# Matmuls of different parts of the TensorE array issued as neighbours in the mixers of a hybrid layer

## The chip, the core and the metric

The kernel runs as one program on one core of a Trainium2 chip. The metric is the device time of one execution in microseconds; less is better. A core has TensorE (matrix products, with an array of 128 rows by 128 columns), VectorE, ScalarE, GpSimd, SyncE (which issues most DMAs) and 16 DMA engines. In the views TensorE's products are PE, its weight loads PEld, VectorE is DVE, ScalarE is ACT, GpSimd is POOL, SyncE is SP. Each engine runs its own instructions in the order in which they were issued to it.

## What is computed

One layer of a diffusion backbone, all in f32: 512 latent tokens and 256 context tokens of width 1024.

```
mod      = silu(c) @ w_mod + b_mod                 # 6 x 1024: shifts, scales, gates
h        = rmsnorm(x) * (1 + sc1) + sh1            # latent and context
cols     = h @ w_in                                # 4480 columns
y_rw     = RWKV-7, 8 heads of 64, both directions  # s = s*w + (s a) b + v k ; y = s r
y_hg     = HGRN2, 8 heads of 64, both directions   # gated linear attention in blocks of 32
x        = x + g1 * (concat(y_rw, y_hg) @ w_out)
h2       = rmsnorm(x) * (1 + sc2) + sh2
x        = x + g2 * (shared SwiGLU(h2) + sum of 8 of 64 routed SwiGLU experts(h2))
out      = rmsnorm(x)
```

Each latent scan begins with the final state of the context scan of its direction.

## The kernel before, in words

Two parts follow one another. The *mixers* take x to `x1` (projection, RWKV-7, HGRN2, output product). The *experts* then route the tokens and stream 64 experts' weights through on-chip buffers.

**The mixers** are generator functions ("streams") that issue instructions step by step; a `yield` ends a step. A planner (`run`) walks over the streams and gives every step a priority worked out from the table `PLAN`: for each stream some due times and, as last number, how many steps it has. A stream's steps are spread evenly over its due times; instructions then stand on each engine in the order of their priorities. The streams are W and P (weight split, projection), E (conv and evacuation), O (RWKV operands), S (RWKV scores, `rw_scores`), I (inverse of small triangles), A, B and C (chains, `rw_chain`), H and K (HGRN2 pairs, `hgrn_pair`), M (rest of the modulation, `s_mod`), N and U (RWKV output, output product).

Heads go in pairs: a tile's 128 partitions hold head 0 of the pair in rows 0 to 63 and head 1 in rows 64 to 127. j counts the four pairs, d the two directions, n the twelve 64-token chunks (4 of context, 8 latent).

- `rw_scores` (L687 matmul, L689 mask and copy on VectorE): for each (j, d) and two chunks, one head after the other: two matmuls of 64 rows, a step; the mask multiply, a step; then the other head; then the DMAs. The two heads use two PSUM banks in turn.
- `rw_chain`: per chunk n, the first product into pR (L888: 64x64 matmuls of W and the scores, two heads; L891: full-height product with the state S, for n > 0), once for each direction; the copy Rs; the U product (L902, direction outside, head inside); the copy W; the state product (L910) and its update; in the latent chunks the output product pY (L926 with S, L928 with W), again once for each direction.
- `hgrn_pair`: for each direction, two groups of 256 tokens and two heads, one step with six matmuls into one bank: p0 (L1115) and p1 (L1116) of 64 rows by 128 columns, p2 (L1118) of 64 by 64, in turn for i = 0 and 1; a step with a predicated copy (L1122); a step with three copies on ScalarE (L1127, L1129). The next head takes the other bank.
- `s_mod`: w_mod's columns 2048 to 6143 in eight blocks m of 512; four loads of 512 KB each (256 rows by 512 columns), and for each load two matmuls of 128 rows by 32 columns on strip g of the array's columns, 512 columns wide.

An f32 matmul stands in the trace as two weight loads and two products; "pieces" are those products.

Of the kernel before, what the change touches and what calls it, by code (L numbers as in the profile page):

```python
# [46 lines left out]
def hybrid_layer(ctx, tc, x, c, xctx, c_ctx, w_mod, b_mod, norm1_g, norm2_g, w_in, rw_conv, rw_w0, rw_w2,  # L47
# [3 lines left out]
    nc = tc.nc  # L51
# [620 lines left out]
    def rw_scores(j, d):  # L672
# [4 lines left out]
        for n in range(0, NCH, 2):  # L677
            lat = n >= NCC
            m = n - NCC if lat else n
            w = WCT[lat]  # L680
            na = w // 64
            st = xq.tile([128, 2, 2, 2, 64], F32, name="SC", bufs=2)
            for h in range(2):
                r = slice(64 * h, 64 * h + 64)
                p3 = pss("p_sc")[:, 0:2 * w].rearrange("p (i t) -> p i t", i=2)
                for i in range(2):
                    pe.matmul(p3[:, i], bk[r, n + i, :], ar[r, n + i, 0:w], start=True, stop=True)  # L687
                yield
                dve.tensor_tensor(st[:, :, 0:na, h], p3.rearrange("p i (a t) -> p i a t", a=na),  # L689
                                  bc(mks[:, d, 0:w].rearrange("p (a t) -> p a t", a=na)[:, None], [128, 2, na, 64]),  # L690
                                  OP.mult)
                yield
            nc.sync.dma_start(SA[rd, n:n + 2], st[rd, :, 0])
            o = 256 + 2 * w + d * 2 * w
            nc.sync.dma_start(PK_d[j, lat][m:m + 2, :, o:o + 2 * w].rearrange("n p c -> p n c"),
                              st[:, :, 0:na].rearrange("p i a h t -> p i (a h t)"))
            yield
# [152 lines left out]
    def rw_chain(j, bank, cp):  # L850
# [20 lines left out]
        for n in range(NCH):  # L871
# [11 lines left out]
            for d in range(2):  # L883
                r = slice(64 * d, 64 * d + 64)
                rv = slice(64 - 64 * d, 128 - 64 * d)
                for h in range(2):
                    o = h * 64
                    pe.matmul(pR[r, o:o + 64], SC[rv, d, 0, h, :], W[rv, d, o:o + 64],  # L888
                              start=(h == 0), stop=(h == 1 and n == 0))
                if n:  # L890
                    pe.matmul(pR[r, 0:128], AR[d][:, 0:64], S[:, d, :], start=False, stop=True)  # L891
# [7 lines left out]
            for d in range(2):  # L899
                r = slice(64 * d, 64 * d + 64)  # L900
                for h in range(2):
# [21 lines left out]
            if lat:  # L923
                for d in range(2):
                    o = d * 64
                    pe.matmul(pY[:, o:o + 64], S[:, d, :], AR[d][:, 64:128], start=True, stop=False)  # L926
                    for h in range(2):
                        pe.matmul(pY[64 * h:64 * h + 64, o:o + 64], W[:, d, h * 64:h * 64 + 64],  # L928
                                  SC[:, d, 1, h, :], start=False, stop=True)
# [77 lines left out]
    def hgrn_pair(j, hq, psg):  # L1007
# [8 lines left out]
        for d in range(2):  # L1016
# [89 lines left out]
            for g in (0, 2):  # L1106
                for h in range(2):
                    r = slice(64 * h, 64 * h + 64)
                    pa = psg("p_ls")
                    p0 = pa[:, 0:256].rearrange("p (g i) -> p g i", g=2)  # L1110
                    p1 = pa[:, 256:384].rearrange("p (g n b) -> p g n b", g=2, n=2)
                    p2 = pa[:, 384:512].rearrange("p (g i) -> p g i", g=2)
                    for i in range(2):
                        gs_ = slice((g + i) * 128, (g + i) * 128 + 128)
                        pe.matmul(p0[:, i], k0_[r, gs_], e1_[r, gs_], start=True, stop=True)  # L1115
                        pe.matmul(p1[:, i], ke_[r, CTX + gs_.start:CTX + gs_.stop], qe4[r, g + i, odd::2, :],  # L1116
                                  start=True, stop=True)
                        pe.matmul(p2[kr_, i], k2[r, g + i].rearrange("p n b -> p (n b)"),  # L1118
                                  q2[r, g + i].rearrange("p n b -> p (n b)"), start=True, stop=True)
                    yield  # L1120
                    Pv = Pg[:, g:g + 2, h, :]
                    dve.copy_predicated(Pv, hgm[d], p0)  # L1122
                    yield
                    for n in range(2):
                        r0 = 64 * n + 32 * (1 - odd)
                        c0 = 64 * n + 32 * odd
                        act.activation(Pv[r0:r0 + 32, :, c0:c0 + 32], p1[r0:r0 + 32, :, n, :], AF.Copy)  # L1127
                    c0 = 32 * qsec
                    act.activation(Pv[kr_, :, c0:c0 + 64], p2[kr_], AF.Copy)  # L1129
                    yield  # L1130
# [46 lines left out]
    def s_mod(psm):  # L1177
# [3 lines left out]
        def loads(i):  # L1181
            if i < 32:
                m, g = 4 + i // 4, i % 4
                wm = mo.tile([128, 2, 512], F32, name="wm2", bufs=3)
                nc.sync.dma_start(wm, dram2(w_mod, m * 512 + g * 256 * 6144, [[6144, 128], [128 * 6144, 2], [1, 512]]))
# [10 lines left out]
        for m in range(4, 12):  # L1196
            pm = psm("p_mod2")
            for g in range(4):
                i = 4 * (m - 4) + g
                loads(i + 2)  # L1200
                yield
                for kt in range(2):
                    pe.matmul(pm[32 * g:32 * g + 32, :], sil[:, 2 * g + kt, :], wms[i][:, kt, :], start=(kt == 0),
                              stop=(kt == 1))
                if g == 1:
# [703 lines left out]
```

## Time and profile before

| | |
|---|---|
| median of three runs | 1876.4 us (1874.18 to 1895.7) |
| the profiled execution | 1872.8 us |
| its span, first to last instruction | 1871.0 us |
| TensorE products busy | 1667.0 us (89% of the span) |
| VectorE, ScalarE, GpSimd busy | 751.0, 618.0, 397.2 us |
| HBM | 212 GB/s over the span |

"Busy" counts the time in which at least one instruction of an engine runs; two products that run beside one another count once. The granted clock of TensorE is a share of 2.4 GHz, and its two levels here are 1 and 0.5 (1.2 GHz); a mean between them tells how a stretch was split. Timeline rows merge neighbours of one kind: the row's time is from the first one's start to the last one's end, which includes a tail of some 0.07 to 0.2 us in which the next group already runs; so the distance from one row's start to the next row's start is the better price.

### The profile page before, as it was taken

How to read it: one execution, taken by the hardware profiler on the slowest of the kernel's cores; microseconds unless marked ns; L12 is line 12 of the kernel's file. 1: busy time of each engine (PE TensorE's matmuls, PEld its weight loads, DVE VectorE, ACT ScalarE, POOL GpSimd, SP SyncE). 2: the span in 40 equal slices, each digit the busy share in tenths (PEclk: the TensorE clock that was granted, in tenths of full speed). 3: DMA queues.
4: the chain of work that ended last, by engine and by line, in shares of the span. 5: the costliest groups of instructions: out<-in, count | busy, mean ns of one | idle time of the engine just before them, and what ended most of it. 6: DMA issues, size and time to landing. Idle time of an engine off the chain costs nothing. (4 is left out here: it accounts for less than half of the span.)

```text
span 1871.0 us, 26459 instructions
## 1 busy us (share of the span) xinstructions
PE 1667.0 (89%) x10155; PEld 994.6 (53%) x10155; DVE 751.0 (40%) x1722; ACT 618.0 (33%) x1286; POOL 397.2 (21%) x372
## 2 busy tenths in 40 slices
PE   5988989999779999989899997988879999999883
PEld 3756677676567776555445543434334544454431
DVE  3665595755847335433344633311112121212113
ACT  5464435426224435342132423321112222222121
POOL 2234222313313124232123011210111111111111
PEclk9976899989867997868799998998889999999997
DMA  7323445546456435453443688799997899999995
GB/s 267 92 59 100 136 136 156 166 112 171 131 152 186 147 119 172 145 171 118 131 146 119 252 302 272 248 322 334 343 302 252 300 339 343 339 328 333 341 340 169
DMA packets 200256, 401.72 MB, mean 215 GB/s; under 512 B 41804, under 2 KB 132009, under 8 KB 175168
## 3 DMA queue, kind: packets, MB, share of 16 engines
q1 hardware_dynamic: 188768, 360.05, 55.9%
q0 software_dynamic: 11360, 39.96, 9.6%
q8 instruction: 81, 1.33, 0.3%
q14 instruction: 47, 0.39, 0.1%
HBM read 323.66 MB, written 73.15 MB: 212 GB/s over the span
## 5 line engine op out<-in xcount | busy, mean ns | idle before, releaser
L1473 PE MATMUL p_gu<-wgu,xT 128*32 128x512 f32 (+2 forms) x1424 | 353.7, 621 | 16.6 <-DMA wgu<-in_exp_w_up_dram 15.9
L1473 PEld LDWEIGHTS p_gu<-wgu,xT 128*32 128x32 f32 (+2 forms) x1424 | 125.9, 143 | 202.4 <-issue 178.9
L1492 PE MATMUL p_y<-wd,at 128*32 128x512 f32 (+2 forms) x744 | 198.0, 621 | 4.8 <-ACT at L1487 3.6
L369 PE MATMUL p_proj<-hTh,w_hi 128*128 128x512 f32 (+1 forms) x456 | 183.3, 402 | 6.0 <-ACT w_hi L296 3.1
L370 PE MATMUL p_proj<-hTh,w_lo 128*128 128x512 f32 (+1 forms) x456 | 177.3, 390 | 3.6 <-DVE w_lo L298 3.6
L371 PE MATMUL p_proj<-hTl,w_hi 128*128 128x512 f32 (+1 forms) x456 | 177.2, 390 | 2.9 <-POOL hTl L351 2.2
L1641 DVE SCALAR_TENSOR_TENSOR li<-lv,bpr 128x2 int32<-128x2 f32 x46 | 10.1, 219 | 411.3 <-DMA acc<-rows,li 299.8
L1694 POOL DMA_INDIRECT acc<-rows,li x46 | 74.3, 1615 | 371.1 <-DVE rows L1693 336.8
L1479 ACT ACTIVATE sl<-p_gu 128x256 f32<-128x256 f32 x50 | 19.1, 383 | 330.5 <-PE p_gu L1473 329.0
L1492 PEld LDWEIGHTS p_y<-wd,at 128*32 128x32 f32 (+2 forms) x744 | 66.3, 147 | 102.1 <-issue 89.2
L1458 ACT ACTIVATE xT<-p_xg,sh2c,s2c 128x128 f32<-128x128 f32 x240 | 89.6, 460 | 91.0 <-PE p_xg L1753 90.8
L369 PEld LDWEIGHTS p_proj<-hTh,w_hi 128*128 128x128 f32 x456 | 94.9, 208 | 28.5 <-issue 6.6
L1693 DVE SCALAR_TENSOR_TENSOR rows<-p_y,lv,g2r 128x512 f32<-128x512 f32 x92 | 67.2, 745 | 100.4 <-PE p_y L1492 100.4
L371 PEld LDWEIGHTS p_proj<-hTl,w_hi 128*128 128x128 f32 x456 | 94.6, 208 | 22.1 <-issue 5.4
L370 PEld LDWEIGHTS p_proj<-hTh,w_lo 128*128 128x128 f32 x456 | 94.7, 208 | 19.5 <-issue 4.9
L1747 POOL DMA_INDIRECT xg<-h,li x30 | 31.0, 1034 | 344.5 <-issue 108.1
L1742 PE MATMUL p_xs<-sel,h2p 128*128 128x128 bf16 x1536 | 92.9, 219 | 0.0
L1742 PEld LDWEIGHTS <-h2p 128*128 128x128 bf16 x1536 | 87.3, 98 | 9.0 <-issue 8.6
L687 PE MATMUL p_sc<-AR,BK 64*128 64x128 f32 (+1 forms) x384 | 64.2, 334 | 20.9 <-DVE SC L689 10.1
L1458 ACT ACTIVATE xT<-p_xs,sh2c,s2c 128x128 f32<-128x128 f32 x128 | 48.1, 457 | 89.9 <-PE p_xs L1742 89.9
L687 PEld LDWEIGHTS p_sc<-AR,BK 64*128 64x128 f32 x384 | 49.8, 221 | 42.4 <-DVE SC L689 14.0
L298 DVE TENSOR_TENSOR w_lo<-w_raw,w_hi 128x1024 fp32r<-128x1024 f32 x35 | 46.3, 1323 | 42.4 <-ACT w_hi L296 42.4
(520 smaller groups left out, 2695.7 us busy)
## 6 DMA issues: line engine op xcount, KB each, us to landing
wgu<-in_exp_w_gate_dram SPq DMA_DIRECT2D x64, 1024.0 KB, 7.5
wgu<-in_exp_w_up_dram SPq DMA_DIRECT2D x64, 1024.0 KB, 7.5
wd<-in_exp_w_down_dram SPq DMA_DIRECT2D x64, 1024.0 KB, 6.4
w_raw<-in_w_in_dram SPq DMA_DIRECT2D x35, 512.0 KB, 4.1
wm<-in_w_mod_dram SPq DMA_DIRECT2D x32, 512.0 KB, 4.0
pkt<-pk SPq DMA_DIRECT2D x24, 576.0 KB, 4.2
wm<-in_w_mod_dram SPq DMA_DIRECT2D x8, 1024.0 KB, 5.2
pk<-SC SPq DMA_DIRECT2D x32, 256.0 KB, 3.1
```

The costliest lines, as they stand in the source:

```text
L298: dve.tensor_tensor(wl, w, wh.bitcast(F32), OP.subtract)
L369: pe.matmul(o[k], wh[:, kt, :], hTh[:, kt, s], start=(kt == 0), stop=False)
L370: pe.matmul(o[k], wl[:, kt, :], hTh[:, kt, s], start=False, stop=False)
L371: pe.matmul(o[k], wh[:, kt, :], hTl[:, kt, s], start=False, stop=(kt == 7))
L687: pe.matmul(p3[:, i], bk[r, n + i, :], ar[r, n + i, 0:w], start=True, stop=True)
L1458: act.activation(dst[:, kt, :], v, AF.Identity, scale=s2c[:, kt:kt + 1], bias=sh2c[:, kt:kt + 1])
L1473: pe.matmul(pg[r], lhs(kt)[:, o:o + r.stop - r.start], w[0][:, :, kt * 256:kt * 256 + 256], start=(kt == 0), stop=(kt == 7))
L1492: pe.matmul(py[n][r], at[:, t * 128 + r.start:t * 128 + r.stop], w[1][:, t * 1024 + n * 512:t * 1024 + n * 512 + 512], start=(t == 0), sto ...
L1693: dve.scalar_tensor_tensor(yo[:, cs_], py[n], g, g2r[:, cs_], op0=OP.mult, op1=OP.mult)
L1694: pool.indirect_dma_start(out=ACC if two else ACC[0:NACC], in_=yo, in_offset=None, compute_op=OP.add, out_offset=bass.IndirectOffsetOnAxis ...
L1742: pe.matmul(pt[:, q * 128:q * 128 + 128], h2p[:, i, t, kt * 128:kt * 128 + 128], sel[:, t], start=(i == 0 and t == 0), stop=(i == 2 and t ...
L1747: pool.indirect_dma_start(out=xg.bitcast(F32), out_offset=None, in_=H2_d, in_offset=bass.IndirectOffsetOnAxis(ap=tok, axis=0))
```

## The change

Four functions issue the same products in another order, and one takes its weights in other blocks.

- `rw_scores`: both heads' matmuls in one step (head innermost), then both mask multiplies in one step.
- `rw_chain`: the first product does the W matmuls of both directions together (direction innermost), then the two S products; the U product has the direction innermost; the output product does both S products, then the four W products.
- `hgrn_pair`: both heads in one step: p0 and p1 of both heads, then p2 of both heads; then both predicated copies; then all copies of ScalarE.
- `s_mod`: a load is 512 rows by 256 columns (rows of 1 KB instead of 2 KB, still 512 KB), and a step has four matmuls of 256 columns, one on each of the four strips.
- `PLAN`: S has 249 steps instead of 345, H and K 129 instead of 153.

```diff
@@ -34,8 +34,8 @@
 PLAN = {'W': (5, 195, 454, 106), 'P': (76, 299, 531, 185), 'E': (31, 271, 489, 172), 'O': (31, 126, 188, 169),
-        'S': (136, 309, 469, 345), 'I': (0, 99, 136, 137), 'A': (247, 419, 623, 201), 'B': (394, 510, 636, 101),
-        'C': (656, 834, 867, 101), 'H': (442, 562, 723, 153), 'K': (531, 677, 962, 153), 'M': (683, 722, 723, 91),
+        'S': (136, 309, 469, 249), 'I': (0, 99, 136, 137), 'A': (247, 419, 623, 201), 'B': (394, 510, 636, 101),
+        'C': (656, 834, 867, 101), 'H': (442, 562, 723, 129), 'K': (531, 677, 962, 129), 'M': (683, 722, 723, 91),
         'U': (1014, 1035, 1193, 91), 'N': (612, 615, 616, 49)}
@@ -680,16 +680,18 @@
             st = xq.tile([128, 2, 2, 2, 64], F32, name="SC", bufs=2)
-            for h in range(2):
-                r = slice(64 * h, 64 * h + 64)
-                p3 = pss("p_sc")[:, 0:2 * w].rearrange("p (i t) -> p i t", i=2)
-                for i in range(2):
+            p3s = [pss("p_sc")[:, 0:2 * w].rearrange("p (i t) -> p i t", i=2) for _ in range(2)]
+            for i in range(2):
+                for h, p3 in enumerate(p3s):
+                    r = slice(64 * h, 64 * h + 64)
                     pe.matmul(p3[:, i], bk[r, n + i, :], ar[r, n + i, 0:w], start=True, stop=True)
-                yield
+            yield
+            for h, p3 in enumerate(p3s):
                 dve.tensor_tensor(st[:, :, 0:na, h], p3.rearrange("p i (a t) -> p i a t", a=na),
...
                                   OP.mult)
-                yield
+            yield
             nc.sync.dma_start(SA[rd, n:n + 2], st[rd, :, 0])
@@ -880,15 +882,17 @@
             W = loaded['W', n // 2][:, n % 2]
-            for d in range(2):
-                r = slice(64 * d, 64 * d + 64)
-                rv = slice(64 - 64 * d, 128 - 64 * d)
-                for h in range(2):
+            for h in range(2):
+                for d in range(2):
+                    r = slice(64 * d, 64 * d + 64)
+                    rv = slice(64 - 64 * d, 128 - 64 * d)
                     o = h * 64
...
                               start=(h == 0), stop=(h == 1 and n == 0))
-                if n:
-                    pe.matmul(pR[r, 0:128], AR[d][:, 0:64], S[:, d, :], start=False, stop=True)
+            if n:
+                for d in range(2):
+                    pe.matmul(pR[64 * d:64 * d + 64, 0:128], AR[d][:, 0:64], S[:, d, :], start=False, stop=True)
             yield
@@ -896,9 +900,9 @@
             yield
-            for d in range(2):
-                r = slice(64 * d, 64 * d + 64)
-                for h in range(2):
+            for h in range(2):
+                for d in range(2):
+                    r = slice(64 * d, 64 * d + 64)
                     pe.matmul(pU[r, h * 64:h * 64 + 64], TT[r, h, :], Rs[r, h * 64:h * 64 + 64],
@@ -921,12 +925,13 @@
                 for d in range(2):
-                    o = d * 64
-                    pe.matmul(pY[:, o:o + 64], S[:, d, :], AR[d][:, 64:128], start=True, stop=False)
+                    pe.matmul(pY[:, d * 64:d * 64 + 64], S[:, d, :], AR[d][:, 64:128], start=(d == 0), stop=False)
+                for d in range(2):
                     for h in range(2):
-                        pe.matmul(pY[64 * h:64 * h + 64, o:o + 64], W[:, d, h * 64:h * 64 + 64],
-                                  SC[:, d, 1, h, :], start=False, stop=True)
+                        pe.matmul(pY[64 * h:64 * h + 64, d * 64:d * 64 + 64], W[:, d, h * 64:h * 64 + 64],
+                                  SC[:, d, 1, h, :], start=False, stop=(d == 1))
                 yield
@@ -1104,30 +1109,36 @@
             for g in (0, 2):
-                for h in range(2):
-                    r = slice(64 * h, 64 * h + 64)
-                    pa = psg("p_ls")
-                    p0 = pa[:, 0:256].rearrange("p (g i) -> p g i", g=2)
-                    p1 = pa[:, 256:384].rearrange("p (g n b) -> p g n b", g=2, n=2)
-                    p2 = pa[:, 384:512].rearrange("p (g i) -> p g i", g=2)
-                    for i in range(2):
-                        gs_ = slice((g + i) * 128, (g + i) * 128 + 128)
+                pas = [psg("p_ls") for _ in range(2)]
+                p0s = [pa[:, 0:256].rearrange("p (g i) -> p g i", g=2) for pa in pas]
+                p1s = [pa[:, 256:384].rearrange("p (g n b) -> p g n b", g=2, n=2) for pa in pas]
+                p2s = [pa[:, 384:512].rearrange("p (g i) -> p g i", g=2) for pa in pas]
+                hr_ = [slice(64 * h, 64 * h + 64) for h in range(2)]
+                for i in range(2):
+                    gs_ = slice((g + i) * 128, (g + i) * 128 + 128)
+                    for r, p0 in zip(hr_, p0s):
                         pe.matmul(p0[:, i], k0_[r, gs_], e1_[r, gs_], start=True, stop=True)
+                    for r, p1 in zip(hr_, p1s):
                         pe.matmul(p1[:, i], ke_[r, CTX + gs_.start:CTX + gs_.stop], qe4[r, g + i, odd::2, :],
                                   start=True, stop=True)
+                for i in range(2):
+                    for r, p2 in zip(hr_, p2s):
                         pe.matmul(p2[kr_, i], k2[r, g + i].rearrange("p n b -> p (n b)"),
                                   q2[r, g + i].rearrange("p n b -> p (n b)"), start=True, stop=True)
-                    yield
+                yield
+                for h in range(2):
+                    dve.copy_predicated(Pg[:, g:g + 2, h, :], hgm[d], p0s[h])
+                yield
+                for h in range(2):
                     Pv = Pg[:, g:g + 2, h, :]
-                    dve.copy_predicated(Pv, hgm[d], p0)
-                    yield
                     for n in range(2):
...
                         c0 = 64 * n + 32 * odd
-                        act.activation(Pv[r0:r0 + 32, :, c0:c0 + 32], p1[r0:r0 + 32, :, n, :], AF.Copy)
+                        act.activation(Pv[r0:r0 + 32, :, c0:c0 + 32], p1s[h][r0:r0 + 32, :, n, :], AF.Copy)
                     c0 = 32 * qsec
-                    act.activation(Pv[kr_, :, c0:c0 + 64], p2[kr_], AF.Copy)
-                    yield
+                    act.activation(Pv[kr_, :, c0:c0 + 64], p2s[h][kr_], AF.Copy)
+                yield
             for i0, i1 in ((0, 3), (3, 5)):
@@ -1180,9 +1191,10 @@
             if i < 32:
-                m, g = 4 + i // 4, i % 4
-                wm = mo.tile([128, 2, 512], F32, name="wm2", bufs=3)
-                nc.sync.dma_start(wm, dram2(w_mod, m * 512 + g * 256 * 6144, [[6144, 128], [128 * 6144, 2], [1, 512]]))
+                m, n, h = 4 + i // 4, i // 2 % 2, i % 2
+                wm = mo.tile([128, 4, 256], F32, name="wm2", bufs=3)
+                nc.sync.dma_start(wm, dram2(w_mod, m * 512 + n * 256 + h * 512 * 6144,
+                                            [[6144, 128], [128 * 6144, 4], [1, 256]]))
                 wms.append(wm)
@@ -1195,14 +1207,14 @@
             pm = psm("p_mod2")
-            for g in range(4):
-                i = 4 * (m - 4) + g
+            for q in range(4):
+                i, n, h = 4 * (m - 4) + q, q // 2, q % 2
                 loads(i + 2)
                 yield
-                for kt in range(2):
-                    pe.matmul(pm[32 * g:32 * g + 32, :], sil[:, 2 * g + kt, :], wms[i][:, kt, :], start=(kt == 0),
-                              stop=(kt == 1))
-                if g == 1:
+                for g in range(4):
+                    pe.matmul(pm[32 * g:32 * g + 32, n * 256:n * 256 + 256], sil[:, 4 * h + g, :], wms[i][:, g, :],
+                              start=(h == 0), stop=(h == 1))
+                if q == 1:
                     store()
...
             mr = mo.tile([128, 512], F32, name="mr2")
```

## Rows read from the trace of the kernel before

**Rows 1.** Windows: stretch, length, busy us (instructions) of PE to POOL, clock, DMA share, GB/s.
```profile
0.00:500.00 500.00, 442.53 (x2561) 319.06 (x2561) 309.64 (x576) 233.08 (x365) 147.62 (x116) 0.90 0.47 137
500.00:1000.00 500.00, 462.50 (x2946) 308.78 (x2947) 219.67 (x508) 173.53 (x385) 129.34 (x170) 0.82 0.47 148
700.00:1000.00 300.00, 281.64 (x1537) 166.29 (x1538) 124.86 (x286) 107.51 (x238) 88.40 (x113) 0.82 0.44 142
1060.00:1871.00 811.00, 703.56 (x4407) 334.05 (x4405) 187.08 (x502) 185.92 (x491) 107.67 (x77) 0.94 0.90 308
```

**Rows 2.** Windows of two stretches of 20 us.
```profile
500.00:520.00 20.00, 10.04 (x46) 7.82 (x46) 18.41 (x48) 1.79 (x3) 4.59 (x3) 0.59 0.65 170
...
840.00:860.00 20.00, 20.00 (x98) 15.41 (x96) 10.68 (x21) 9.00 (x19) 11.18 (x13) 0.63 0.31 109
```

**Rows 3.** Timeline of PE (start us, us, engine, line, ...): scores, together and single.
```profile
194.41 0.72 PE L687 MATMUL p_sc<-AR,BK 64*128 64x128 f32 x8
195.06 0.49 PE L369 MATMUL p_proj<-hTh,w_hi 128*128 128x512 f32 x1
...
205.59 0.71 PE L687 MATMUL p_sc<-AR,BK 64*128 64x128 f32 x4
206.23 0.50 PE L369 MATMUL p_proj<-hTh,w_hi 128*128 128x512 f32 x1
```

**Rows 4.** Timeline of PE, one chain step's first product.
```profile
791.09 0.44 PE L888 MATMUL p_chain<-Wv,pkt 64*64 64x64 f32 x4
791.46 0.43 PE L891 MATMUL p_chain<-S,pkt 128*64 128x128 f32 x2
791.82 0.44 PE L888 MATMUL p_chain<-Wv,pkt 64*64 64x64 f32 x4
792.55 0.62 PE L1203 MATMUL p_mod<-wm,sil 128*32 128x512 f32 x1
```

**Rows 5.** Timeline of PE, a U product and the group after it.
```profile
795.55 0.46 PE L902 MATMUL p_chain<-Rs,pkt 64*64 64x64 f32 x8
795.94 0.38 PE L1134 MATMUL p_kv<-Vt,k3t 128*128 128x128 f32 x1
```

**Rows 6.** Timeline of PE, a chain step's output product and what follows.
```profile
787.15 0.43 PE L926 MATMUL p_chain<-pkt,S 128*128 128x64 f32 x2
...
788.41 0.59 PE L1212 MATMUL p_row<-mr,sel 128*1 128x512 f32 x1
```

**Rows 7.** Timeline of PE, HGRN scores of one head, and what follows.
```profile
796.58 0.48 PE L1115 MATMUL p_ls<-e,k 64*128 64x128 f32 x2
...
798.26 0.32 PE L926 MATMUL p_chain<-pkt,S 128*128 128x64 f32 x1
```

**Rows 8.** Timeline of one modulation step and an expert's strips; between them, all modulation.
```profile
785.32 1.90 PE L1203 MATMUL p_mod<-wm,sil 128*32 128x512 f32 x4
...
L1203 PE MATMUL p_mod<-wm,sil 128*32 128x512 f32 x128 | 50.6, 786 | 3.2 <-DMA wm<-in_w_mod_dram 3.0 <-DVE y_rw L962 0.2
...
1499.87 3.21 PE L1492 MATMUL p_y<-wd,at 128*32 128x512 f32 x28
```

**Rows 9.** DMA issues: count, KB each, median us to landing; wm of L1185, w_raw.
```profile
w_raw<-in_w_in_dram SPq DMA_DIRECT2D x35, 512.0 KB, 4.1
wm<-in_w_mod_dram SPq DMA_DIRECT2D x32, 512.0 KB, 4.0
```

**Rows 10.** Waits in 530 to 1010 (us, times, longest); reads by line (ns min/median/max).
```profile
DVE Pg L1122 <- PE p_ls L1118: 67.3, 27, 7.3
...
L1122 DVE COPY_PREDICATED Pg<-hgm,p_ls x32: 441/444/450, 607.8 to 993.5; 128x256 f32<-128x256 uint8 x32
...
L1129 ACT ACTIVATE Pg<-p_ls x32: 258/272/272, 608.7 to 994.5; 64x128 f32<-64x128 f32 x32
...
L689 DVE TENSOR_TENSOR SC<-p_sc,mks x96: 272/412/427, 126.2 to 528.0; 128x256 f32<-128x256 f32 x64, 128x128 f32<-128x128 f32 x32
```

**Rows 11.** Timeline of PE, the last output product before the second norm.
```profile
1034.30 1.02 PE L1269 MATMUL p_out<-wol,y_rw 128*128 128x512 f32 x2
```

## The prediction, made before the changed kernel had run

> **What bounds the kernel now.** I read busy time and clock by stretch first [rows 1, 2]. TensorE is busy 442 of the first 500 us and 462 of the next, the next engine (VectorE) 310 and 220; no other engine sets the pace of this part for long. From 1060 us on the DMA engines are at 0.90: that part streams expert weights, the change does not touch it, and it starts when the mixers end. So a microsecond off the mixers is a microsecond off the run, and in the mixers TensorE is to be relieved. Two things stand against a full return. VectorE has stretches of its own: in 500 to 520 it is busy 18.4 of 20 and TensorE 10.0 [rows 2]. And TensorE's granted clock is 0.90 and 0.82 in the two halves [rows 1]. With levels at 1 and 0.5, a mean of 0.86 puts 280 us of the first 1000 at 1.2 GHz, and the same work at full clock would take 860 us.
>
> Then the timeline of TensorE, one group of matmuls at a time. Each f32 matmul is two pieces there. A group's price is the time from its start to the next group's start, all at full clock.
>
> **The change part by part.**
>
> *Scores.* One head's four pieces take 205.59 to 206.23, 0.64 us. Where both heads happen to stand together, eight pieces take 194.41 to 195.06, 0.65 us [rows 3]: the other half of the rows runs beside, for nothing. So a pair that becomes one group saves 0.63 us. Of 48 pairs (8 rounds of 6), 14 already stand as eight in the timeline and six more follow one another in the last round; 28 are split. 28 x 0.63 = 18 us.
>
> *Chain, first product.* Now a step goes through the array twice: W of one direction, S of it, then the same for the other, 791.09 to 792.55, 1.46 us, with four changes of shape on the way [rows 4]. Afterwards the eight W pieces stand together. Nearest row: the U product, eight pieces of the same 64x64 form on opposite quadrants, 795.55 to 795.94, 0.39 us [rows 5]. The two S products use different column halves; one takes 791.46 to 791.82, 0.36, and the second runs beside it. Price 0.75, saving 0.71 in each of 11 steps of four chains: 31 us.
>
> *Chain, U product.* Order only. Its eight pieces take 0.39 us although the old order issues both matmuls of one quadrant before the other's, as long as four pieces of the W product alone (0.37) [rows 4, 5]. So they overlap already, and I cost this at nothing. The Trainium skill (TensorE: Matmul & The Clock Gate, Part 3, The mechanism) says that matmuls keep program order strictly; by that the new order would free up to half of 0.39 us in 48 steps, some 9 us more. This trace disagrees, and the sum goes by the row.
>
> *Chain, output product.* Two directions take 787.15 to 788.41, 1.26 us [rows 6]. Afterwards the two full-array products stand together and the four half-width ones too: one shape change in and one out go away. The bounds are 0 and 0.63 (a direction wholly hidden); the full-array half cannot overlap with itself, so I take 0.30. 8 x 4 x 0.30 = 10 us.
>
> *HGRN scores.* One head and group pair takes 796.58 to 798.26, 1.68 us, and changes shape four times because the 64x64 product stands between 64x128 ones [rows 7]. Both heads now: 3.36. Afterwards 16 pieces in the 64x128 form, two at a time (twice the score pair, 1.30) and eight in the 64x64 form (the U row, 0.39): 1.69. Saving 1.67 x 16 = 27 us.
>
> *Modulation.* A step's four pieces of 512 columns on one strip of 32 take 785.32 to 787.15, 1.83 us [rows 6, 8]; all 32 steps are busy 50.6 us, so some overlap already. Afterwards a step has eight pieces of 256 columns on four strips. The expert row does 28 pieces of 512 columns on four strips in 3.21 us, 0.115 each [rows 8], so 8 x 0.057 = 0.46; a short group pays more for its change of shape, and I take 0.5. At the 0.82 clock of this part [rows 1] that is 0.61, x 32 = 20; saving 31 us there, 25 at full clock. Its loads become rows of 1 KB in place of 2 KB. The same 512 KB land in 4.0 us with 2 KB rows and in 4.1 us with the 512 B rows of the projection weights [rows 9], so I cost them at nothing; SyncE issues as many as before.
>
> *Steps and plan.* S, H and K lose the steps that the merging took away, so each stream keeps its pace against the others. No evacuation is added: VectorE and ScalarE do the same, in pairs.
>
> **The sum.** 18 + 31 + 10 + 27 + 25 = 111 us of TensorE at full clock; over 0.86, 129 us of this run. Not all comes back. TensorE runs in issue order, and a shorter stretch uncovers latencies of ScalarE, VectorE and GpSimd between dependent steps. Of the saving, the scores and about a third of the chains lie before 530 us, where VectorE is busy 62% and has saturated stretches; the larger part lies in 530 to 1000, where VectorE is at 44% and waits for TensorE: the predicated copies alone 67.3 us [rows 10]. I let a third of the first part and two thirds of the second return, together 60%: 77 us. The mixers then end near 958 us in place of 1035 [rows 11]. The profiled execution took 1872.8 us around its span of 1871.0, 0.2% under the median of 1876.4; I count from the median: 1799.
>
> **The rivals.**
>
> *Evacuation becomes the wait.* Both PSUM banks of a stream now fill at once and must both be read before the next group; before, one was read while the other filled. Price: an HGRN pair's reads are two of VectorE at 0.444 and six of ScalarE, at most 0.272 each, 2.52 us; a score pair's two at 0.41 [rows 10]. If TensorE stood for all of it, 16 x 2.52 + 28 x 0.82 = 63 us; the run would gain 77 - 63 = 14, 1862. Against it: between two groups of a stream the plan puts matmuls of three to five others, and today it is the readers that wait. The Trainium skill (TensorEngine Tiling (Array Packing), PSUM Bottleneck) says that packing speeds up TensorE but not the reading of PSUM, which may become the limit. So far this trace shows the opposite, the 67.3 us in which readers wait. Half of this price gives about 1830.
>
> *The clock gives it back: slower.* The place is 500 to 1000 us. There the clock falls although TensorE counts as busy: 0.63 in 840 to 860 with 20.0 of 20 [rows 2], a stretch of small chain and score products, and 0.82 over 700 to 1000 [rows 1]. The long modulation products, 1.83 us without a break, are the densest work in them, and the change makes them 0.5. In full-clock terms the mixers' first 1000 us take 860 - 111 + H/2, H being the time at 1.2 GHz. H is 280 now; no gain at 502, over 2% slower beyond 577. If all from 500 on stayed at 1.2 GHz: 500 x 0.82 = 410, less the 79 saved there, 331, doubled 662, against 500; less 36 saved before. That is +126, 2002 us. Against it: the projections until 700 and the output product after 850 keep their long products, and the gaps between packed groups shrink too.
>
> *The overlap does not come.* Then only changes of shape are saved. No row parts them from the pieces; between none and half of the 111 us, 60% of the middle is 17: 1859. The pairs that overlap already speak against it [rows 3, 5].
>
> **How the numbers follow.** Forecast (30 to 130 us off): 0.68. A larger gain, if the clock rises with denser work: 0.06. Evacuation or other waits eat most, 1835 to 1870: 0.15. No overlap: 0.03. Clock: 0.08, 0.01 of it only to no change. About 37 us, 2%, is what this kernel's runs (1874 to 1896) can tell from no change. Of the forecast's share 0.63 lies beyond it, with the larger gain and 0.02 of the evacuation case, so faster 0.71; within 2%, 0.22; slower 0.07. The range is 1745, where all 129 return, to 1850, where the waits take most; it leaves the clock case and the far half of the evacuation case out.
>
> **What would show it.** Scores: groups of eight in about 0.65 us, no fours. Chain: W eight and S four pieces together, 0.75. HGRN: one group per two heads in about 1.7 us. Modulation busy about 20 us. The last output product ends near 958 us, and the stretch behind it is as long as before. The forecast is wrong if TensorE's idle time before 1000 us grows from 95 to well over 150, if the clock of 700 to 1000 falls below 0.70, or if the waits on the HGRN reads turn from TensorE's readers to TensorE.

## The result, and the profile after

The changed kernel takes 1815.5 us (median of four runs, 1800.4 to 1821.1), the kernel before 1879.1 beside it: ratio 0.9634, 95% interval 0.9548 to 0.972, or 64 us less. The forecast was 1799, in a range of 1745 to 1850. The profiled execution took 1812.1 us.

The page's totals, busy us and share of the span:

```profile
span 1810.3 us, 26679 instructions
PE 1583.8 (87%) x10283; PEld 955.5 (53%) x10283; DVE 754.0 (42%) x1722; ACT 620.9 (34%) x1289; POOL 392.3 (22%) x372
```

TensorE's products fell from 1667.0 to 1583.8 us; no other engine changed by more than 5. Windows by stretch, columns as in [rows 1]:

```profile
0.00:500.00 500.00, 439.48 (x2549) 316.68 (x2549) 316.40 (x586) 237.74 (x368) 142.69 (x116) 0.86 0.48 138
500.00:1000.00 500.00, 440.23 (x3314) 305.33 (x3315) 246.75 (x611) 196.09 (x427) 141.84 (x180) 0.82 0.51 163
700.00:1000.00 300.00, 267.46 (x1901) 165.72 (x1902) 157.65 (x401) 129.48 (x280) 97.58 (x123) 0.87 0.52 175
```

The mean clock of the first half fell from 0.90 to 0.86; that of the second stayed at 0.82. The timeline of PE gives the new prices, against [rows 3 to 8]: a pair of scores that stands together, one that does not, a chain's first product, a U product, an output product, an HGRN group of two heads, and one head that stands alone with a modulation step behind it.

```profile
234.70 0.66 PE L688 MATMUL p_sc<-AR,BK 64*128 64x64 f32 x8
235.29 0.39 PE L369 MATMUL p_proj<-hTh,w_hi 128*128 128x256 f32 x1
...
206.28 0.69 PE L688 MATMUL p_sc<-AR,BK 64*128 64x128 f32 x4
206.90 0.50 PE L369 MATMUL p_proj<-hTh,w_hi 128*128 128x512 f32 x1
...
743.21 0.45 PE L891 MATMUL p_chain<-Wv,pkt 64*64 64x64 f32 x8
743.59 0.44 PE L895 MATMUL p_chain<-S,pkt 128*64 128x128 f32 x4
743.96 0.44 PE L391 MATMUL p_tok<-ident,k 128*128 128x128 f32 x2
...
672.25 0.45 PE L906 MATMUL p_chain<-Rs,pkt 64*64 64x64 f32 x8
672.63 0.50 PE L369 MATMUL p_proj<-hTh,w_hi 128*128 128x512 f32 x1
...
740.55 0.56 PE L930 MATMUL p_chain<-pkt,S 128*128 128x64 f32 x4
741.03 0.45 PE L933 MATMUL p_chain<-pkt,Wv 128*64 128x64 f32 x8
741.32 0.39 PE L1164 MATMUL p_o<-Pg,Vt 128*64 128x128 f32 x4
...
688.68 0.49 PE L1121 MATMUL p_ls<-e,k 64*128 64x128 f32 x4
...
689.72 0.45 PE L1127 MATMUL p_ls<-q,k 64*64 64x64 f32 x8
690.10 0.50 PE L369 MATMUL p_proj<-hTh,w_hi 128*128 128x512 f32 x1
...
745.08 0.48 PE L1121 MATMUL p_ls<-e,k 64*128 64x128 f32 x2
...
746.11 0.44 PE L1127 MATMUL p_ls<-q,k 64*64 64x64 f32 x4
746.48 0.64 PE L1215 MATMUL p_mod<-wm,sil 128*32 128x256 f32 x8
747.05 0.45 PE L906 MATMUL p_chain<-Rs,pkt 64*64 64x64 f32 x8
```

The first product takes 743.21 to 743.96, 0.75 us where it took 1.46; U 0.38 as before; the output product 0.77 where it took 1.26; two HGRN heads 688.68 to 690.10, 1.42 where one took 1.68; a modulation step 0.57. But at 206.28 one head's four score pieces still stand alone, for 0.62 us, and at 745.08 one HGRN head, half of the pieces of a group, for 1.40. That row parts two effects: the same 12 pieces of one head cost 0.28 us less by the order of their shapes alone, and the second head, where it stands beside, adds 0.02. The groups by line say the same (busy us, mean ns | idle before, released by):

```profile
L688 PE MATMUL p_sc<-AR,BK 64*128 64x128 f32 (+1 forms) x384 | 65.9, 368 | 23.1 <-DVE SC L691 12.1 <-POOL BK L637 6.6 <-DVE BK L638 4.4
L1215 PE MATMUL p_mod<-wm,sil 128*32 128x256 f32 x256 | 23.9, 441 | 2.0 <-DMA wm<-in_w_mod_dram 1.9
```

Modulation went from 50.6 to 23.9 us busy; the scores' products went from 64.2 to 65.9, not down. The last output product, and the predicated copies' wait for TensorE before it (470 to 960 us):

```profile
972.86 1.02 PE L1281 MATMUL p_out<-wol,y_rw 128*128 128x512 f32 x2
973.72 1.04 PE L1524 MATMUL p_h<-ident,h 128*128 128x128 f32 x8
...
DVE Pg L1131 <- PE p_ls L1127: 25.0, 13, 5.7
```

The mixers end at 973.9 instead of 1035.3 [rows 11]: 61 us earlier. The stretch behind them took 836.4 us against 835.7. So all of the gain is in the mixers.

**One table for all runs.** A clock record says when TensorE ran at 1.2 GHz. "Full-clock length" is the mixers' end less half of the time at 1.2 GHz ahead of it: a shorter end comes from less length or from less slow time. All but the ratios are from the profiled execution, in us.

| kernel | ratio to before [95%] | mixers end | at 1.2 GHz | full-clock length | behind |
|---|---|---|---|---|---|
| before | 1 | 1035.3 | 283 | 894 | 835.7 |
| the change | 0.9634 [0.9548, 0.972] | 973.9 | 317 | 815 | 836.4 |
| e1 scores only | 1.0144 [1.0068, 1.022] | 1072.7 | 406 | 870 | 840.0 |
| e2 all but scores | 0.9581 [0.9518, 0.9644] | 955.9 | 263 | 824 | 857.6 |
| e3 HGRN only | 0.9866 [0.98, 0.9932] | 991.3 | 236 | 874 | 856.8 |
| e4 chain only | 0.9784 [0.9709, 0.986] | 1003.6 | 287 | 860 | 844.8 |
| e5 scores, forced pairs | 0.9964 [0.9916, 1.0012] | 1023.6 | 294 | 877 | 838.5 |
| e6 scores, old step count | 0.9993 [0.9932, 1.0055] | 1061.0 | 362 | 880 | 836.3 |
| e7 modulation only | 1.0098 [1.0042, 1.0154] | 1024.3 | 314 | 867 | 837.5 |
| e8 change, old U order | 0.9714 [0.9638, 0.979] | 969.6 | 317 | 811 | 858.5 |
| e9 change, reads twice | 0.9741 [0.9675, 0.9808] | 976.6 | 307 | 823 | 850.4 |
| e10 change, forced pairs | 0.9428 [0.9369, 0.9487] | 929.0 | 239 | 810 | 839.0 |
| e11 chain and HGRN | 0.9602 [0.954, 0.9664] | 962.3 | 232 | 846 | 851.5 |
| e12 scores forced, twice | 1.0192 [1.0122, 1.0263] | 1056.4 | 317 | 898 | 834.2 |

The stretch behind runs the same instructions in all of them and still varies by 24 us, so one profile of a kernel is worth no more than that against another; the ratios rest on several runs each. They leave out executions more than 1.5% over their kernel's shortest, which is at most one of each variant's four to ten, but five of ten in e6 and e7.

Every execution has its span (first to last instruction) and its mean granted clock on record, so the two sums can be had for each, over the whole span: time at 1.2 GHz is 2 x (1 - clock) x span, full-clock length clock x span. The clock is on record to 0.001, which is 2 us of length. Medians (lowest to highest), all executions, us:

| kernel | executions | full-clock length | at 1.2 GHz |
|---|---|---|---|
| before, beside the variants | 43 | 1680 (1671 to 1689) | 398 (354 to 435) |
| the change | 4 | 1603 (1602 to 1604) | 423 (388 to 433) |
| e1 scores only | 4 | 1665 (1654 to 1671) | 488 (486 to 505) |
| e2 all but scores | 4 | 1617 (1610 to 1623) | 381 (353 to 394) |
| e3 HGRN only | 4 | 1664 (1657 to 1672) | 383 (362 to 393) |
| e4 chain only | 4 | 1649 (1642 to 1651) | 392 (367 to 407) |
| e5 scores, forced pairs | 10 | 1667 (1656 to 1678) | 407 (387 to 440) |
| e6 scores, old step count | 10 | 1669 (1666 to 1674) | 460 (393 to 490) |
| e7 modulation only | 10 | 1653 (1642 to 1668) | 471 (424 to 535) |
| e8 change, old U order | 4 | 1604 (1601 to 1609) | 444 (438 to 462) |
| e9 change, reads twice | 4 | 1614 (1609 to 1620) | 431 (417 to 445) |
| e10 change, forced pairs | 6 | 1598 (1595 to 1606) | 347 (320 to 353) |
| e11 chain and HGRN | 6 | 1635 (1624 to 1641) | 346 (333 to 408) |
| e12 scores forced, twice | 4 | 1686 (1681 to 1688) | 449 (420 to 473) |

From one execution to the next a kernel's length moves little (2 to 26 us), its slow time more (19 to 111). Over the 43 executions of before, a microsecond more at 1.2 GHz goes with 0.44 us more of span, so the half that the tables take is near what slow time costs.

### The profile page after: what moved, and what is told of

Same layout as the page of the kernel before. It is cut to its first block, busy times and chain, and to the rows that moved or that the text cites. A ratio compares the mean times of both kernels' runs of the same rounds, so it can differ in the third digit from the quotient of the medians.

```text
span 1810.3 us, 26679 instructions
## 1 busy us (share of the span) xinstructions
PE 1583.8 (87%) x10283; PEld 955.5 (53%) x10283; DVE 754.0 (42%) x1722; ACT 620.9 (34%) x1289; POOL 392.3 (22%) x372
## 5 line engine op out<-in xcount | busy, mean ns | idle before, releaser
L1504 PEld LDWEIGHTS p_y<-wd,at 128*32 128x32 f32 (+2 forms) x744 | 65.9, 147 | 102.3 <-issue 89.2
L369 PEld LDWEIGHTS p_proj<-hTh,w_hi 128*128 128x128 f32 x456 | 93.8, 206 | 28.2 <-issue 8.3
L1705 DVE SCALAR_TENSOR_TENSOR rows<-p_y,lv,g2r 128x512 f32<-128x512 f32 x92 | 67.3, 745 | 95.8 <-PE p_y L1504 95.8
L688 PE MATMUL p_sc<-AR,BK 64*128 64x128 f32 (+1 forms) x384 | 65.9, 368 | 23.1 <-DVE SC L691 12.1
```

What stands on the lines that cost most here:

```text
L369: pe.matmul(o[k], wh[:, kt, :], hTh[:, kt, s], start=(kt == 0), stop=False)
L1504: pe.matmul(py[n][r], at[:, t * 128 + r.start:t * 128 + r.stop], w[1][:, t * 1024 + n * 512:t * 1024 + n * 512 + 512], start=(t == 0), sto ...
L1705: dve.scalar_tensor_tensor(yo[:, cs_], py[n], g, g2r[:, cs_], op0=OP.mult, op1=OP.mult)
```

## The experiments

**e1 and e2: the scores edit alone, and all the rest without it.** e1 takes the hunk of `rw_scores` and this line; e2 takes every other hunk.

```diff
-        'S': (136, 309, 469, 345), 'I': (0, 99, 136, 137), 'A': (247, 419, 623, 201), 'B': (394, 510, 636, 101),
+        'S': (136, 309, 469, 249), 'I': (0, 99, 136, 137), 'A': (247, 419, 623, 201), 'B': (394, 510, 636, 101),
```

> The kernel before with the edit of rw_scores alone (S with 249 steps). By the prediction's step, every pair becomes one group: 18 us of TensorE at full clock, of which a third returns, so 5 to 8 us faster, about 1870. By the rival (the two banks come free one after the other and the pairs fall apart again in issue order, while both banks now fill at once) nothing or a loss: 1875 to 1890, with score groups of four still the more frequent form and scores busy at 64 us or more. In the changed kernel 22 groups stand as eight, with the joined ones at the end some 30 of 48 pairs, against 20 before.

> The changed kernel with rw_scores as before (S with 345 steps). If the scores part carries its share, this loses 5 to 8 us against the whole change: about 1821. If the scores part brings nothing or costs, this equals or beats the whole change: 1800 to 1815.

The edit alone made the kernel slower, 1915.0 us against 1883.8 and outside both of its bands; the rest alone took 1806.0 (0.9581), as good as the whole. The scores' products are 66.1 us busy, 30 groups of four stand against 28 of eight: the pairs fall apart, as the rival had it. But that alone would cost nothing: in the first table e1's full-clock length falls by 24 us, and 123 us more are spent at 1.2 GHz. Over all executions it is 15 less and 90 more, and no execution of before has as much slow time as any of e1. Windows of e1, then of before (PE busy, clock, DMA share, GB/s):

```profile
500.00:700.00 200.00, 172.33 (x1236) 0.68 0.49 144
600.00:640.00 40.00, 36.70 (x217) 0.54 0.35 102
```

```profile
500.00:700.00 200.00, 180.86 (x1411) 0.82 0.53 156
600.00:640.00 40.00, 40.00 (x394) 0.96 0.53 150
```

In these 200 us the projection's long products stand beside small ones in both; e1 runs them at 0.68, before at 0.82.

**e3 and e4: the HGRN edit alone, the chain edits alone (all three products).** e3 takes the hunk of `hgrn_pair` and the line below, e4 the three hunks of `rw_chain` and the old line.

```diff
-        'C': (656, 834, 867, 101), 'H': (442, 562, 723, 153), 'K': (531, 677, 962, 153), 'M': (683, 722, 723, 91),
+        'C': (656, 834, 867, 101), 'H': (442, 562, 723, 129), 'K': (531, 677, 962, 129), 'M': (683, 722, 723, 91),
```

> The kernel before with the edit of hgrn_pair alone (H and K with 129 steps). The groups of HGRN scores fall from 64 us in all to about 34, as in the changed kernel. If TensorE's time sets the pace, some two thirds return: 17 to 24 us faster, 1855 to 1862. If the reading of the two banks becomes the wait (rival), the gain is under 8 us and TensorE shows waits on ScalarE or VectorE ahead of the score groups.

> The kernel before with the three edits of rw_chain alone. First product 79 to 51 us in all, output product 43 to 36, U product unchanged: 35 us of TensorE time. With TensorE setting the pace two thirds return, 20 to 26 us faster, 1852 to 1860. If the chains' own latency or the clock takes it, under 10 us.

Of 1879, the ratios are 25 and 41 us less, just above e3's forecast (17 to 24) and well above e4's (20 to 26). Both shorten the full-clock length, by 20 and 34 us in the profiles, 16 and 31 over all executions; these two edits carry the change, as e11 will show.

**e5: scores, with each pair held together.** Head 0's first matmul waits for the last reader of the bank that head 1 will take (`pss_rd` lists these readers); the other three follow at once.

```diff
+                    if i == 0 and h == 1:
+                        pr, tc.cur_priority = tc.cur_priority, tc.cur_priority - 20000
-                    pe.matmul(p3[:, i], bk[r, n + i, :], ar[r, n + i, 0:w], start=True, stop=True)
+                    mm = pe.matmul(p3[:, i], bk[r, n + i, :], ar[r, n + i, 0:w], start=True, stop=True)
+                    if i == h == 0:
+                        first = mm.ins
+                        if pss_rd:
+                            tc.add_manual_dep(first, pss_rd[-1].name, mybir.DependencyInfo(
...
+                    else:
+                        tc.add_manual_dep(mm.ins, first.name, mybir.DependencyInfo(
...
```

> The kernel before with the scores edit alone, and each pair forced to stand together: head 0's first matmul waits until both PSUM banks are free, and the other three follow it at once. Theory A (the edit fails because pairs fall apart: some 30 of 48 joined): with nearly all 48 joined the products of this line fall from 65 us busy to some 45, the granted clock stays at 0.89 or above, and the run is 0.990 to 0.997 of the time before. Theory B (what costs is the joining itself, since TensorE does less in the stretch and the clock falls further): clock of 300 to 700 us below 0.80 as in the scores edit alone, run 1.01 to 1.03. Theory C (both banks free at once is the cost: TensorE waits for VectorE): TensorE's idle time in the first 700 us grows by over 20 us at an unchanged clock, run 1.005 to 1.02.

In the trace 45 groups of eight now stand without another product between, 28 in e1; the scores' group of e1, then of e5:

```profile
L688 PE MATMUL p_sc<-AR,BK 64*128 64x128 f32 (+1 forms) x384 | 66.1, 365 | 21.3 <-DVE SC L691 11.8 <-POOL BK L637 5.1 <-DVE BK L638 4.4
```

```profile
L692 PE MATMUL p_sc<-AR,BK 64*128 64x128 f32 (+1 forms) x384 | 42.4, 339 | 23.9 <-DVE SC L704 16.1 <-POOL BK L637 3.4 <-ACT KBs L729 2.6
```

66.1 us busy became 42.4, as theory A asked, and the run's clock is A's too (0.892). TensorE's idle time in the first 700 us is 91.5 us against 76.6 before, so theory C's 20 did not come. The loss of e1 is gone: 0.9964, and slow time is back at 407 us. But the interval reaches 1, and the granted clock in 300 to 500 and 500 to 700 was 0.85 and 0.81, between A and B. The edit changes the wait, the order and the priority of the other three at once, so it does not show which of these joins the pairs.

**e6: scores, with S's 345 steps kept** by an empty step behind the matmuls and one behind the multiplies.

```diff
                     pe.matmul(p3[:, i], bk[r, n + i, :], ar[r, n + i, 0:w], start=True, stop=True)
             yield
+            yield
```

> The scores edit alone, but stream S keeps its 345 steps: an empty step stands behind the matmuls and one behind the mask multiplies, so that its DMAs come at the old pace. Theory A (the order of the steps in the plan made the scores edit alone slow, not the joining): 0.995 to 1.003 of the time before, and the clock of 300 to 700 us comes back to 0.85 or more. Theory B (the joining, in whatever place, costs clock): 1.010 to 1.020 as the scores edit alone, clock of 300 to 700 about 0.77.

The ratio 0.9993 is what theory A said, but it rests on five of ten executions. The median of all ten is 1901.6 us against 1879.8, 1.2% more and in theory B's band, and the clock of 300 to 500 and 500 to 700 came only to 0.84 and 0.81. Slow time, 460 us, lies between e5's 407 and e1's 488 and goes from 393 to 490. So the run does not decide between the theories; that the pace of the steps alone made e1 slow is not shown.

**e7: the modulation edit alone** (the two hunks of `s_mod`).

```diff
-                wm = mo.tile([128, 2, 512], F32, name="wm2", bufs=3)
+                wm = mo.tile([128, 4, 256], F32, name="wm2", bufs=3)
```

> The modulation edit alone (loads of 512 rows by 256 columns, four products on four strips in a step). The prediction's step gives 25 us at full clock and 60 per cent of 29 returned, 18 us: 0.990. What the other single edits leave of the change without the scores (78 less 25 less 40) is 13 us: 0.993. The rival that the clock gives it back: the clock of 700 to 850 us falls below 0.73 and the run is 1.00 or more, though the products of this line are busy 25 us in place of 50.

No gain: 1.0098, and a median of 1893.3 us against 1879.8 over all ten executions. The products of the line fell to 27.7 us and the full-clock length by 27, but the clock of 700 to 850 fell, before and then e7:

```profile
700.00:850.00 150.00, 140.83 (x820) 91.64 (x821) 63.55 (x154) 67.84 (x141) 51.34 (x72) 0.73 0.48 158
```

```profile
700.00:850.00 150.00, 141.99 (x803) 99.28 (x801) 63.63 (x149) 66.79 (x143) 50.14 (x72) 0.61 0.46 152
```

TensorE is as busy, at 0.61 instead of 0.73: the slower rival, for this part of the change. The profile fell on the shortest of e7's ten executions (1863.7 us), in which the mixers even end 11 us earlier than before, so it cannot show the loss itself. All ten can: 27 us less of length, 73 us more at 1.2 GHz, which by halves is some 10 us lost.

**e8: the change with the old U order.**

```diff
-            for h in range(2):
-                for d in range(2):
-                    r = slice(64 * d, 64 * d + 64)
+            for d in range(2):
+                r = slice(64 * d, 64 * d + 64)
+                for h in range(2):
```

> The whole change, but the U product in its old order (direction outside, head inside). By the row of before (eight pieces in 0.39 us in the old order) nothing changes: 0.960 to 0.967 of the time before, and the eight pieces take 0.39 to 0.45 us. If matmuls of one quadrant hold back those of the other, the eight take 0.6 us or more in the old order against 0.4 in the new, 48 times 0.2 to 0.4, some 10 to 15 us: 0.969 to 0.972.

```profile
663.67 0.46 PE L906 MATMUL p_chain<-Rs,pkt 64*64 64x64 f32 x8
664.06 0.50 PE L369 MATMUL p_proj<-hTh,w_hi 128*128 128x512 f32 x1
```

Eight pieces take 0.39 us, against 0.38 in the new order; all U products come to 25.1 and 25.4 us at full clock. The ratio (0.9714) lies in the band of the theory that holds pieces back, but the mixers end no later (969.6); in the profile 22 us lie in the stretch behind, which the order does not touch, and the intervals overlap. Over all executions the lengths are 1604 and 1603 us. The order costs nothing.

**e9: the change with every read of the merged banks done twice.**

```diff
                     dve.copy_predicated(Pg[:, g:g + 2, h, :], hgm[d], p0s[h])
+                    dve.copy_predicated(Pg[:, g:g + 2, h, :], hgm[d], p0s[h])
```

> The whole change, with every read of the merged banks done twice: the mask multiplies of the scores, the predicated copies and ScalarE's copies of HGRN2. That adds 96 x 0.41 + 32 x 0.44 = 53 us to VectorE and 96 x at most 0.27 = 26 us to ScalarE. Forecast (readers wait for TensorE, not the other way): at most 15 us more, 0.963 to 0.972 of the time before. Rival (TensorE stands for the reads of a pair): 48 x 0.82 + 16 x 2.5 = 80 us more, 1.00 or above.

1829.3 us, 14 more than the change (20 by the ratios), where the evacuation rival needed 80. The ratio 0.9741 is just above the forecast's band. Even with doubled reads the mixers end 3 us later only, and the full-clock length over all executions is 11 us more.

**e10: the change with e5's forced pairs.**

```diff
+                        if pss_rd:
+                            tc.add_manual_dep(first, pss_rd[-1].name, mybir.DependencyInfo(
...
```

> The whole change, and each pair of scores forced to stand together as in the earlier run of the scores alone. If the prediction's term for the scores (18 us at full clock) comes once the pairs are joined: products of that line 42 us busy in place of 66 and 0.950 to 0.958 of the time before. If the clock takes it back, as with the scores alone: the same 42 us busy, but the time at 1.2 GHz before the mixers' end rises above 317 us and the run stays at 0.960 to 0.970.

The fastest kernel: 1772.5 us, 0.9428, its interval apart from those of the change and of e2. The scores' products are 41.6 us busy. The size was better than either theory, and for a reason that neither had: full-clock length fell by 5 us only, and time at 1.2 GHz by 78. All executions say the same: 5 us of length, and 320 to 353 us at 1.2 GHz where the change has 388 to 433. Windows of the change, then of e10:

```profile
500.00:600.00 100.00, 74.44 (x632) 58.94 (x632) 61.45 (x156) 29.46 (x61) 28.13 (x32) 0.67 0.62 175
600.00:640.00 40.00, 40.00 (x311) 31.55 (x310) 9.17 (x24) 13.39 (x32) 5.32 (x5) 0.50 0.30 87
```

```profile
500.00:600.00 100.00, 86.40 (x744) 68.14 (x745) 55.67 (x129) 40.35 (x83) 23.63 (x28) 0.87 0.59 171
600.00:640.00 40.00, 39.16 (x322) 31.98 (x321) 15.57 (x30) 17.92 (x42) 11.97 (x19) 1.00 0.48 152
```

**e11: chain and HGRN edits, scores and modulation as before.** Against e2, `s_mod` goes back.

```diff
-                wm = mo.tile([128, 4, 256], F32, name="wm2", bufs=3)
+                wm = mo.tile([128, 2, 512], F32, name="wm2", bufs=3)
```

> Chain (all three products) and HGRN2 edits together, with the scores and the modulation as before. If the modulation edit costs time in company too, as alone (1.01): 0.945 to 0.955. If what the two edits give alone just adds (25 and 40 us): 0.965. If the modulation edit pays in company: 0.965 to 0.975, above the 0.958 of the kernel that has it.

0.9602, between two of its bands, against e2's 0.9581, which adds the modulation edit, and the change's 0.9634: no difference. The modulation edit takes 22 us off the length (846 to 824) and adds 31 us at 1.2 GHz; over all executions 18 and 35.

**e12: e5 with each pair's products issued twice.**

```diff
-            for i in range(2):
+            for i in (0, 1, 2, 3):
```

> The kernel before with the scores edit and forced pairs, each pair's eight products issued twice into the same banks: 48 x 0.6 = 29 us more of TensorE at full clock than the forced pairs alone (0.996), no new reads. If TensorE's work alone sets the time: 1.010 to 1.016. If the time at 1.2 GHz falls when the engine has more to do (the clock had taken back what the pairs saved): at most 1.003, and time at 1.2 GHz before the mixers' end below 260 us against 294.

1.0192, beyond the band of work alone (1.010 to 1.016, of which its interval covers the upper part): the full-clock length rose by 21 us against e5, and the slow time did not fall but rose by 23 (over all executions 19 and 42). So the clock does not simply pay back added work of this kind.

## Why the prediction was right, and where it was not

**The terms.** For each product I summed start to next start over all groups, each multiplied by its granted clock (us at full clock, idle time behind a group included; the modulation includes 16 us of its first four blocks, which are unchanged):

| term | forecast | before | after | saved |
|---|---|---|---|---|
| scores | 18 | 57.9 | 50.2 | 8 |
| chain, first product | 31 | 65.0 | 39.8 | 25 |
| chain, U | 0 | 23.7 | 25.4 | -2 |
| chain, output product | 10 | 40.5 | 30.5 | 10 |
| HGRN scores | 27 | 50.8 | 28.2 | 23 |
| modulation | 25 | 53.2 | 37.3 | 16 |

They add to 80, and the full-clock length of the mixers fell by 79. The forecast was 111.

**The step that failed: that the 28 split pairs become one group.** Standing in one step did not make the matmuls neighbours. In the traces 28 groups of eight stand without another product between, 20 did before, and 30 groups of four are left, where the prediction's sign was "no fours". That the second head waits for a bank that frees later is the likely reason, not shown by itself. The price of a group was right: with the pairs forced together (e5) 45 groups of eight stand, and the line falls from 57.9 to 35.0 us at full clock, 23, more than the 18.

**Terms mis-sized.** Modulation: I turned its 50.6 us busy into full clock with the 0.82 of 700 to 1000; its own stretch, 700 to 850, ran at 0.73, so there was less to save (37 us at full clock, not 41), and a step costs 0.57, not 0.50, or 0.66 with the idle time behind it (21.2 us for 32 steps). HGRN and the chain's first product are 4 and 6 us under, though a whole group costs what was forecast or less (1.42 for 1.69, 0.75 for 0.75): in the timeline groups are still split by other streams' products; of the 16 HGRN groups 7 stand whole, and a head alone costs 1.40. U was put at nothing, and nothing came (2 us more).

**How much returns.** I had 40% of the saving lost to uncovered latencies (43% by the prediction's own weights: a third of 32 us and two thirds of 79 are 63 of 111). TensorE's idle time before the mixers' end did rise, from 96 to 118 us, but it is inside the 79. What took back the rest was the clock: 34 us more at 1.2 GHz cost 17 by halves, and 79 - 17 is the 61 of the mixers within 1 us. It is 12 if slow time with an idle TensorE costs nothing: TensorE was busy in 284 of the 317 us, before in 260 of 283. So the total was near (1799 forecast, 1815.5 measured; mixers' end 958 and 973.9) partly by luck: less work was saved than forecast, and more of it returned (61 of 79, forecast 77 of 111).

**The rivals.** Evacuation: refuted by e9 and by the readers' wait, 25.0 us after against 67.3 [rows 10], still on their side. No overlap: refuted by the 0.75 and by two HGRN heads in 1.42, one in 1.40. The clock: by the prediction's own formula slow time would have had to grow by twice 79 us for no gain; it grew by 34, and not where the rival looked: the clock of 500 to 1000 us stayed at 0.82, that of the first half fell. It did decide two of the parts: scores alone (90 us more over all executions) and modulation alone (73 more) ended slower than before.

**What stays open.** Which property of the order sets the slow time. In the profiles of these kernels it goes from 232 to 406 us ahead of the mixers' end, worth up to 87 us of run, and not with the work saved: e1 and e5 have the same length over all executions (1665, 1667) and 81 us between their slow times. So of e10's gain over the change, 39 of its 45 us in the mixers come from slow time, and the runs do not say that another kernel would get them.

## What to carry to other kernels

Price a TensorE edit in two sums, work at full clock and time at the low clock, each from the stretch where the edit lies; the first came to within a third of its forecast, the second could not be forecast. Take both from several executions: span and mean clock of each give them. Putting matmuls into one step does not make them neighbours: look at the order in the trace; here it took a wait of the first for both banks, with the others tied to it at a higher priority, to join them. Try the parts of a change singly and without each: here one part lost by itself, one gave nothing, and the first one, once its pairs were held together, went with the best kernel.

## What the runs showed of the hardware

- TensorE can stay at 1.2 GHz while it counts as fully busy: in the change 600 to 640 us are 40.00 of 40 busy at 0.50, after 100 us with 74.44 busy at 0.67; in e10 the same stretch is 39.16 busy at 1.00, after 86.40 at 0.87.
- How long TensorE stays at 1.2 GHz differs between executions of the same kernel: 354 to 435 us in 43 executions of before, 393 to 490 in ten of e6, at a full-clock length that moves by 18 and 8 us.
- Products on opposite 64x64 quadrants overlap in either issue order: eight pieces in 0.39 and 0.38 us, where four took 0.37 [rows 4]. The Trainium skill (TensorE: Matmul & The Clock Gate, Part 3, The mechanism) has matmuls start strictly in program order; no row here shows a cost of it. Nor does a row show that the order is broken, as the prediction read it: the rows show only that it costs no time here.
- An HGRN head's 12 pieces take 1.68 us with the 64x64 ones in two places [rows 7], 1.40 with them at the end, and two heads so together 1.42.
- Eight half-height score pieces on both row halves take 0.65 us, four on one half 0.64 [rows 3]; of the 64x64 form, eight take 0.59 (234.70 in the change) and four 0.585 (227.54 before). The second half of the array is free, if its work is there.
